# Where the second product of a SwiGLU block loads its first weights, when its operands are split, and which banks end its last token tile

## The chip, the cores and the metric

The kernel runs on one core of a Trainium2 chip. The metric is device time in microseconds of one execution, given as the median of several runs. On a core work five engines with instruction queues of their own, each in order: TensorE (PE, matmul, with PEld for the loading of its stationary operand), VectorE (DVE), ScalarE (ACT), GpSimd (POOL) and SyncE (SP, which here only issues DMA). They meet through semaphores.

## The reference, cut to what matters

One decoder block on x of 512 tokens by 1024 columns, in float32: a mixer (RWKV-7, MoBA attention and gMLP heads) and then a SwiGLU FFN with 2816 hidden columns. The change touches the end of the FFN alone:

```python
h = rmsnorm(x, pre_ffn_g[l])
gate, up = jnp.split(h @ w_ffn_in[l], 2, axis=-1)      # 512 x 2816 each
f = (jax.nn.silu(gate) * up) @ w_ffn_out[l]            # 512 x 1024: the second product
x = x + rmsnorm(f, post_ffn_g[l])
```

## The kernel before, in words

**Exactness.** Each float32 operand is split into a high part (rounded to the matmul's type, copied by ACT) and a low part (the rest, a subtraction on DVE). A product is three matmuls: high by high, high by low, low by high (`mm3`). Names that end in h and l are these parts: `wh`, `wl` of weights, `fh`, `fl` of whole blocks of f, `xh`, `xl` of quarter pieces of f.

**First product.** It makes f transposed, 22 blocks of 128 hidden columns by 512 tokens. From block 3 on, each block is computed by `seven(b, between)` with seven half-size products in place of eight, and the last part of block b (`finish`, lines 1351 to 1354: add, Silu, multiply) runs inside block b+1 as `between`. Blocks 0 to 3 are split at once into `fh` and `fl`. Blocks 4 to 21 stay whole in `bigh`, `bigl` and `fx`.

**Second product.** Its 22 rows of f blocks are in two groups. Blocks 0 to 9 are multiplied plainly, as five units of two blocks (`NU = 5`). Blocks 10 to 21 go through a scheme that replaces eight block products by seven (`product2` with the names p1 to p7, three steps u = 0, 1, 2 each). Column half 512:1024 comes first, in the order unit 0, 1, 2, 3, p1, p5, p6, unit 4, p7, p4; then half 0:512 with p2, p3 and units 0 to 4, the last three of which run token tile by token tile with `finish2` behind each tile. A unit is 24 matmuls of 128x512, a p is 36 (12 for each u).

**Weights of a step.** `w2_load` (line 1399) issues a DMA of 512 KB on SP's queue into a tile `wf`; the pools in `sp_tiles` are taken in turn, each with two buffers. `w2_parts` then copies the high part on ACT (line 1405) and subtracts the low part on DVE (line 1406). In `operands`, p5 to p3 first add or subtract two weight tiles or pieces of f on DVE (lines 1447 to 1467; `sw` is the running sum of weights, `t2` that of f) and split what they need of f into `xh` (ACT, line 1432) and `xl` (DVE, line 1433).

**Pools.** `wpool` is the old pool: the first product's weights went through it too. `fo` (the pool "out") is opened after unit 0, on memory that the first product gives back, so its first tiles wait for the last readers of that memory. Right behind `fo` the kernel appends it to `sp_tiles`, so that unit 1 loads into `wpool`, unit 2 into `fo`, unit 3 into `wpool`, p1's first step into `fo` and so on.

**Order.** PE runs in the order of the code. The other engines' instructions are placed by a list scheduler: what stands under `tc.high_priority(offset=PRI_W)` is taken as if it stood 20,000 instructions earlier. The weights' loads and splits, and those of the pieces of f, stand under it. `to_parts(b, fr[b])` for blocks 4 to 9 (lines 1277, 1278) stands in the loop over units, without precedence.

**End.** `finish2` (t is the token tile) adds the bank to what was kept in `s1` or `u2` (line 1544), squares and sums on ACT (1522), multiplies by the gain (1546), sums the squares (1549, 1551), takes the power on POOL (1554), updates x2 (1556, twice) and sends it out. The last tile, t = 3, is done in two column cuts of 256, both in the same bank `c1[1]`.

Of the kernel before, what the change touches and what calls it, by code (L numbers as in the profile page):

```python
# [12 lines left out]
OP = mybir.AluOpType  # L13
# [5 lines left out]
NB = S // 128  # L19
# [21 lines left out]
PRI_W = 20000  # L41
# [55 lines left out]
def block_kernel(ctx: ExitStack, tc: tile.TileContext, x, pre_mix_g, w_in, rwkv_mu, rwkv_w0, rwkv_w2,  # L97
# [4 lines left out]
    act, dve, pool, sp = nc.scalar, nc.vector, nc.gpsimd, nc.sync  # L102
# [22 lines left out]
    def bank(name, bufs):  # L125
        return ps.tile([128, 512], F32, name=name, bufs=bufs)

    def acc():
        return bank("acc", 2)

    def rb():
        return bank("rb", 1)

    def yb():
        return bank("yb", 1)

    def sb():
        return bank("sb", 3)
# [7 lines left out]
    def ct(shape, name, dt=F32):  # L146
        return const.tile(shape, dt, name=name)
# [244 lines left out]
    for h in range(2):  # L392
        r = slice(64 * h, 64 * h + 64)
# [74 lines left out]
    def dense_fm(free=False):  # L468

        wh, wl = feed.next()  # L470
        wh = wh.rearrange("p (k c) -> p k c", k=KB)
        wl = wl.rearrange("p (k c) -> p k c", k=KB)
        p = acc()
        for k in range(KB):
            pe.matmul(p, wh[:, k], h1[:, k], start=(k == 0), stop=False)
            pe.matmul(p, wh[:, k], l1[:, k], start=False, stop=False)
            pe.matmul(p, wl[:, k], h1[:, k], start=False, stop=(k == KB - 1))
            if free:
                od.signal("free%d" % k)
            if k < KB - 1:  # L480
                od.pump()
        return p
# [529 lines left out]
    p = dense_fm()  # L1012
# [8 lines left out]
    u2 = bkt[:, 16:24].rearrange("p u m -> p (u m)").rearrange("p (b s) -> p b s", b=2)  # L1021
# [13 lines left out]
    for b in range(2):  # L1035
        p = dense_fm(b == 1)
# [62 lines left out]
    sm = ct([128, 3 * NB], "sm")  # L1099
# [102 lines left out]
    K1, K2 = FB - 2 * NW, FB - NW  # L1202
# [9 lines left out]
    def ffn_w():  # L1212
        return tuple(w.rearrange("p (k c) -> p k c", k=KB) for w in ffeed.next())

    ws = [ffn_w() for _ in range(4)]
# [38 lines left out]
    ws = [ffn_w() for _ in range(2)]  # L1254
# [10 lines left out]
    FA = 4  # L1265
# [4 lines left out]
    fr = [h1f[:, i] for i in range(KB)] + [l1f[:, i] for i in range(KB)] + [fx[:, i] for i in range(FB - FA - 2 * KB)]  # L1270
    fr = [None] * FA + fr
# [4 lines left out]
    def to_parts(b, f):  # L1276
        act.copy(fh[b], f)
        dve.tensor_tensor(fl[b], f, fh[b].bitcast(F32), op=OP.subtract)
# [110 lines left out]
    sp_tiles, w_tiles, w2 = [wpool], [0, 0], w_ffn_out[0].rearrange("(k p) c -> p k c", p=128)  # L1389
# [19 lines left out]
    def mm3(p, ah, al, wh, wl, start, stop):  # L1409
        pe.matmul(p, ah, wh, start=start, stop=False, skip_group_check=True)  # L1410
        pe.matmul(p, ah, wl, start=False, stop=False, skip_group_check=True)
        pe.matmul(p, al, wh, start=False, stop=stop, skip_group_check=True)

    def plain_w(ui, c):
        with tc.high_priority(offset=PRI_W):
            return w2_parts(w2_load(2 * ui, c))

    def plain(ui, w, p, t, start=False, cut=slice(0, 512)):
        tk = slice(128 * t, 128 * t + 128)
        for kk in range(2):  # L1420
            b = 2 * ui + kk
            mm3(p[:, cut], fh[b][:, tk], fl[b][:, tk], w[0][:, kk, cut], w[1][:, kk, cut], start and kk == 0, kk == 1)
# [13 lines left out]
    def operands(name, u):  # L1436

        ka, kb = K1 + 2 * u, K2 + 2 * u
        b11, b12, b21, b22 = rows(ka, 0), rows(ka, 1), rows(kb, 0), rows(kb, 1)
        t2, sw = st2["t2"][u], st2["sw"][u]  # L1440
        t2v = t2.rearrange("p (k c) -> p k c", k=2)
        if name == "p1":
            a, x = w2_load(ka, 0), b11
        elif name == "p5":
            a, x = w2_load(ka, 512), b12
            other = w2_load(kb, 512)
            dve.tensor_tensor(sw, a, other, op=OP.add)  # L1447
            a = sw
        elif name == "p6":
            a = w2_load(ka, 0)  # L1450
            dve.tensor_tensor(sw, sw, a, op=OP.subtract)
            dve.tensor_tensor(t2v, b22, b12, op=OP.subtract)
            a, x = sw, t2v
        elif name == "p7":
            a, other = w2_load(ka, 0), w2_load(ka, 512)
            dve.tensor_tensor(a, a, other, op=OP.subtract)
            dve.tensor_tensor(b11, t2v, b11, op=OP.subtract)
            x = b11
        elif name == "p4":
            a = w2_load(kb, 512)  # L1460
            dve.tensor_tensor(t2v, b21, t2v, op=OP.subtract)
            x = t2v
        elif name == "p2":
            a, x = w2_load(kb, 0), b21
        else:
            a, x = w2_load(kb, 0), b22
            dve.tensor_tensor(a, a, sw, op=OP.subtract)
        return w2_parts(a), f_parts(x)

    def product2(name, ps_, start=False):  # L1470

        for u in range(NW // 2):
            with tc.high_priority(offset=PRI_W):
                w, x = operands(name, u)
            for t in range(2):
                tk = slice(128 * t, 128 * t + 128)
                for kk in range(2):
                    mm3(ps_[t], x[0][:, kk, tk], x[1][:, kk, tk], w[0][:, kk], w[1][:, kk], start and u == kk == 0,
                        u == NW // 2 - 1 and kk == 1)

    def keep_banks(name, ps_):
        with tc.high_priority(offset=2 * PRI_W):
            d = u3 if name == "u3" else st2["fo"].tile([128, 2, 512], F32, name=name)
            for t in range(2):
                act.copy(d[:, t], ps_[t])
        return d

    NU = K1 // 2
    c0, cd = (rb(), yb()), (ob(), sb())
    for ui in range(NU - 1):  # L1490
        w = plain_w(ui, 512)
        for t in range(NB):
            plain(ui, w, (c0 + cd)[t], t, ui == 0)
        if ui == 0:
            between()
            ffs.close()
            hps.close()
            fo = st2["fo"] = ph2.enter_context(tc.tile_pool(name="out", bufs=1, reuse_waits="tile"))
            sp_tiles.append(fo)
            for b in range(FA, K1):  # L1500
                fh.append(fo.tile([128, S], F32R, name="fh%d" % b))
                fl.append(fo.tile([128, S], F32R, name="fl%d" % b))
                to_parts(b, fr[b])
            st2["t2"] = [fo.tile([128, 512], F32, name="t2_%d" % u) for u in range(NW // 2)]
            st2["sw"] = [fo.tile([128, 1024], F32, name="sw%d" % u) for u in range(NW // 2)]
            raw = fo.tile([128, NB, 512], F32, name="raw")
    cb, c1 = (acc(), acc()), (sb(), sb())
    product2("p1", cb, True)
    s1 = keep_banks("s1", cb)
    product2("p5", c1, True)  # L1510
    product2("p6", cb)
    u2 = keep_banks("u2", cb)
    w = plain_w(NU - 1, 512)
# [22 lines left out]
    ca_ = (acc(), acc())  # L1536
    product2("p2", ca_, True)
    product2("p3", c1)

    def finish2(t, cut, last):  # L1540

        e = (s1, u2)[t // 2][:, t % 2]
        i = 3 * t + (1 if cut.start == 0 else 2)
        dve.tensor_tensor(e[:, cut], (ca_ + c1)[t][:, cut], e[:, cut], op=OP.add)
        square_sum(e[:, cut], i)
        dve.tensor_tensor(e[:, cut], e[:, cut], orow[:, cut], op=OP.mult)
        r = rs[:, t:t + 1]
        if cut.start == 0:
            dve.scalar_tensor_tensor(r, sm[:, i - 1:i], 1e-6, sm[:, i:i + 1], op0=OP.add, op1=OP.add)  # L1549
        else:  # L1550
            dve.tensor_tensor(r, r, sm[:, i:i + 1], op=OP.add)
        if not last:
            return
        pool.tensor_tensor(r, r, mhalf[:, 0:1], op=OP.pow)  # L1554
        for c, src in ((slice(512, D), raw[:, t]), (slice(0, 512), e)):
            dve.scalar_tensor_tensor(x2[:, t, c], src, r, x2[:, t, c], op0=OP.mult, op1=OP.add)  # L1556
            sp.dma_start(out_rows[:, t, c], x2[:, t, c])

    ws = []
    for ui in range(NU):  # L1560
        ws.append(plain_w(ui, 0))
        if ui < NU - 3:
            for t in range(NB):
                plain(ui, ws[ui], (ca_ + c1)[t], t)
    for t in range(NB):
        cuts = [slice(0, 512)] if t < NB - 1 else [slice(0, 256), slice(256, 512)]
        for cut in cuts:
            for ui in range(NU - 3, NU):
                plain(ui, ws[ui], (ca_ + c1)[t], t, False, cut)
            finish2(t, cut, cut is cuts[-1])  # L1570
    inner.close()
    ph2.close()

# [28 lines left out]
```

## Time and profile before

| what | us |
| --- | --- |
| runs | 655.35, 655.42, 657.01 |
| median | 655.42 |
| the profiled execution | 656.08 |
| its span, first to last instruction | 654.4 |
| PE busy | 631.9 (97%) |
| DVE busy | 490.0 (75%) |
| ACT busy | 326.3 (50%) |
| mean granted TensorE clock | 0.990 of full speed |

The span is the time between the first and the last instruction of the profiled execution; 1.68 us of that execution lie outside it. A busy PE means that matmuls are under way, at whichever clock; the granted clock says how fast. Of two matmuls with the same shape the difference of their starts is the time that one takes from the stream, since they overlap in the pipeline.

### The profile page before, as it was taken

The page shows a single profiled execution, that of the slowest core. Times are in us where ns is not written, and L with a number is a line of the kernel's source. Part 1 is how long each engine was busy: PE and PEld are TensorE (multiplying, and loading weights), DVE is VectorE, ACT ScalarE, POOL GpSimd, SP SyncE. Part 2 cuts the span into 40 slices and gives each one's busy share as a digit, 9 for nine tenths or more (in the row PEclk, how much of TensorE's full clock was granted, in tenths as well). Part 3 has the DMA queues.
Part 4 walks back from the last instruction along what each step waited for, and adds up shares of the span by engine and source line. Part 5 has one row for each costly group of instructions (what it writes and reads, how often), then busy time and mean ns, then how long its engine had stood idle before and what let it go on. Part 6 is the DMA issues. An engine that isn't in the chain of part 4 may idle for free.

```text
span 654.4 us, 11566 instructions
## 1 busy us (share of the span) xinstructions
PE 631.9 (97%) x4582; PEld 559.4 (85%) x4582; DVE 490.0 (75%) x834; ACT 326.3 (50%) x582; POOL 59.5 (9%) x111
## 2 busy tenths in 40 slices
PE   8998999999999999999999999999999978999995
PEld 7886879877878887789999999999999967788884
DVE  2799969886565768468988888888888565889825
ACT  6653543455554463456755455555455351646511
POOL 7021121032130100022000000000000000000001
PEclk9999999999999999999999999999999998999999
DMA  7422012321211126406333243343342144856503
GB/s 228 132 69 66 25 48 78 108 67 46 58 33 33 34 65 258 135 26 189 102 97 115 81 127 99 96 130 97 98 124 71 37 157 161 263 171 209 161 0 129
DMA packets 84981, 69.12 MB, mean 106 GB/s; under 512 B 2968, under 2 KB 70976, under 8 KB 84928
## 3 DMA queue, kind: packets, MB, share of 16 engines
q1 hardware_dynamic: 83024, 65.76, 32.4%
q10 hardware_dynamic: 1904, 2.63, 1.3%
q8 instruction: 36, 0.59, 0.4%
q14 instruction: 17, 0.14, 0.1%
HBM read 66.28 MB, written 2.10 MB: 104 GB/s over the span
## 4 chain that ended last, share of the span: by engine, by line
PE 68%; DVE 9%; DMA 4%; issue 2%; ACT 1%; POOL 0%; DVEq 0%; POOLq 0%; ACTq 0%
PE acc L112 30%; PE sb L112 27%; PE rb L112 4%; PE yb L112 3%; DMA wf<-in_w_ffn_out_dram 3%; PE ob L112 3%; PE sb L117 1%; DVE wl L185 1%; DMA wf<-in_w_out_dram 1%; DVE wl L1406 1%; ACT wh L183 1%; DVE sw L1447 1%; DVE xl L1433 1%; DVE x L1556 1%; DVE bigl L814 0%
## 5 line engine op out<-in xcount | busy, mean ns | idle before, releaser
L112 PE MATMUL sb<-h,wh 128*128 128x256 f32 x260 | 73.5, 283 | 0.0
L112 PE MATMUL sb<-h,wl 128*128 128x256 f32 x260 | 73.4, 282 | 0.0
L112 PE MATMUL sb<-l,wh 128*128 128x256 f32 x260 | 73.3, 282 | 0.0
L112 PE MATMUL acc<-bigh,wh 128*128 128x512 f32 (+1 forms) x168 | 67.0, 402 | 0.3 <-ACT bigh L281 0.3
L112 PE MATMUL acc<-bigl,wh 128*128 128x512 f32 (+1 forms) x168 | 63.6, 383 | 0.3
L183 ACT ACTIVATE wh<-wf 128x512 fp32r<-128x512 f32 (+2 forms) x60 | 40.4, 711 | 45.6 <-PE acc L112 31.6
L185 DVE TENSOR_TENSOR wl<-wf,wh 128x512 fp32r<-128x512 f32 (+2 forms) x60 | 46.6, 799 | 19.2 <-ACT wh L183 17.2
L112 PE MATMUL acc<-bigh,wl 128*128 128x512 f32 (+1 forms) x168 | 59.3, 377 | 0.0
L1313 ACT ACTIVATE wh<-wf 128x1024 fp32r<-128x1024 f32 x38 | 40.1, 1059 | 33.5 <-DVE wf L1334 16.0
L1314 DVE TENSOR_TENSOR wl<-wf,wh 128x1024 fp32r<-128x1024 f32 x38 | 46.0, 1222 | 9.6 <-ACT wh L1313 9.6
L112 PEld LDWEIGHTS sb<-l,wh 128*128 128x128 f32 x260 | 49.5, 190 | 0.0
L112 PEld LDWEIGHTS sb<-h,wh 128*128 128x128 f32 x260 | 49.5, 190 | 0.0
L112 PEld LDWEIGHTS sb<-h,wl 128*128 128x128 f32 x260 | 49.5, 190 | 0.0
L1405 ACT ACTIVATE wh<-wf 128x1024 fp32r<-128x1024 f32 x25 | 26.1, 1057 | 37.0 <-PE sb L112 29.9
L112 PEld LDWEIGHTS acc<-bigh,wh 128*128 128x128 f32 x168 | 32.0, 190 | 6.0 <-ACT bigh L281 0.6
L112 PEld LDWEIGHTS acc<-bigl,wh 128*128 128x128 f32 x168 | 31.9, 190 | 5.8 <-DVE bigl L282 0.9
L1406 DVE TENSOR_TENSOR wl<-wf,wh 128x1024 fp32r<-128x1024 f32 x25 | 30.1, 1218 | 8.2 <-ACT wh L1405 8.1
L1313 ACT ACTIVATE wh<-sums 128x1024 fp32r<-128x1024 f32 x19 | 20.1, 1060 | 31.7 <-PE acc L112 16.4
L112 PEld LDWEIGHTS acc<-bigh,wl 128*128 128x128 f32 x168 | 30.0, 189 | 6.2
L1554 POOL TENSOR_TENSOR rs<-rs,mhalf 128x1 f32<-128x1 f32 x4 | 2.2, 549 | 343.1 <-DVE rs L1549 339.3
L1314 DVE TENSOR_TENSOR wl<-sums,wh 128x1024 fp32r<-128x1024 f32 x19 | 23.2, 1223 | 13.2 <-ACT wh L1313 13.2
L112 PE MATMUL acc<-l,wh 128*128 128x256 f32 x108 | 30.5, 283 | 0.9 <-DVE l L1187 0.9
(489 smaller groups left out, 1906.8 us busy)
## 6 DMA issues: line engine op xcount, KB each, us to landing
wf<-in_w_ffn_in_dram SPq DMA_DIRECT2D x76, 256.0 KB
wf<-in_w_ffn_out_dram SPq DMA_DIRECT2D x37, 512.0 KB
wf<-in_w_in_dram SPq DMA_DIRECT2D x21, 512.0 KB
wf<-in_w_out_dram SPq DMA_DIRECT2D x8, 512.0 KB
wf<-in_w_ffn_in_dram SPq DMA_DIRECT2D x6, 512.0 KB
xt<-in_x_dram SPq DMA_DIRECT2D x4, 512.0 KB
x<-in_x_dram SPq DMA_DIRECT2D x4, 512.0 KB
out_dram<-x SPq DMA_DIRECT2D x8, 256.0 KB
```

The lines of the kernel that those rows point to most:

```text
L112: return nc.tensor.matmul(out_, lhsT, rhs, **kw)
L117: return nc.tensor.transpose(out_, in_, idn)
L183: act.activation(h[:, c], t[:, c], AF.Copy)
L185: eng.tensor_tensor(l[:, c], t[:, c], h[:, c].bitcast(F32), op=OP.subtract)
L1313: act.activation(h, src, AF.Copy)
L1314: dve.tensor_tensor(l, src, h.bitcast(F32), op=OP.subtract)
L1405: act.activation(h, src, AF.Copy)
L1406: dve.tensor_tensor(l, src, h.bitcast(F32), op=OP.subtract)
L1433: dve.tensor_tensor(l, src, h.bitcast(F32), op=OP.subtract)
L1447: dve.tensor_tensor(sw, a, other, op=OP.add)
L1554: pool.tensor_tensor(r, r, mhalf[:, 0:1], op=OP.pow)
L1556: dve.scalar_tensor_tensor(x2[:, t, c], src, r, x2[:, t, c], op0=OP.mult, op1=OP.add)
```

## The change

Three edits, all in the second product.

1. `sp_tiles.append(fo)` moves out of the loop over units, behind it. Units 0 to 3 thus all load into `wpool`; `fo` takes part from p1 on.
2. `to_parts` of blocks 4 to 7 (the f blocks of units 2 and 3) gets the precedence PRI_W, ahead of the splits of p1's pieces in the code. Blocks 8 and 9 (unit 4) are split behind `product2("p5")` in the code, with the same precedence.
3. The last three units of token tile 3 no longer add to bank `c1[1]`: the first column cut starts a sum of its own in a bank from `rb()`, the second in one from `yb()`. What the earlier work left in `c1[1]` is added to `u2[:, 1]` by one new DVE instruction (line 1571 after the change) ahead of the loop over tiles. The line that adds the second cut's square sum moves within `finish2`.

```diff
-            sp_tiles.append(fo)
             for b in range(FA, K1):
                 fh.append(fo.tile([128, S], F32R, name="fh%d" % b))
                 fl.append(fo.tile([128, S], F32R, name="fl%d" % b))
-                to_parts(b, fr[b])
+            with tc.high_priority(offset=PRI_W):
+                for b in range(FA, 2 * NU - 2):
+                    to_parts(b, fr[b])
...
+    sp_tiles.append(fo)
     cb, c1 = (acc(), acc()), (sb(), sb())
     product2("p1", cb, True)
     s1 = keep_banks("s1", cb)
     product2("p5", c1, True)
+    with tc.high_priority(offset=PRI_W):
+        for b in range(2 * NU - 2, K1):
+            to_parts(b, fr[b])
     product2("p6", cb)
...
-    def finish2(t, cut, last):
+    def finish2(t, p, cut, last):
...
-        dve.tensor_tensor(e[:, cut], (ca_ + c1)[t][:, cut], e[:, cut], op=OP.add)
+        dve.tensor_tensor(e[:, cut], p[:, cut], e[:, cut], op=OP.add)
...
+    with tc.high_priority(offset=PRI_W):
+        dve.tensor_tensor(u2[:, 1], c1[1], u2[:, 1], op=OP.add)
     for t in range(NB):
-        cuts = [slice(0, 512)] if t < NB - 1 else [slice(0, 256), slice(256, 512)]
-        for cut in cuts:
+        end = t == NB - 1
+        cuts = [slice(0, 256), slice(256, 512)] if end else [slice(0, 512)]
+        for cut, p in zip(cuts, (rb(), yb()) if end else (ca_ + c1)[t:t + 1]):
             for ui in range(NU - 3, NU):
-                plain(ui, ws[ui], (ca_ + c1)[t], t, False, cut)
-            finish2(t, cut, cut is cuts[-1])
+                plain(ui, ws[ui], p, t, end and ui == NU - 3, cut)
+            finish2(t, p, cut, cut is cuts[-1])
```

Lines behind the first edit have other numbers after the change: `finish2`'s 1544, 1546, 1549, 1551, 1556 become 1549, 1551, 1554, 1558, 1561.

**SP's queue, the loads of units 1 to 3 and of p1 and p5.** Before (wf_5993 is unit 1, wf_6053 unit 3, wf_6023 unit 2, wf_6087, wf_6109 and wf_6131 are p1's three steps, wf_6156 and wf_6158 the pair of p5's first step, wf_6181 and wf_6183 that of its second):

```order
L1399 DMA wf_5993<-in_w_ffn_out_dram 128x2x512
L1399 DMA wf_6053<-in_w_ffn_out_dram 128x2x512
L1399 DMA wf_6109<-in_w_ffn_out_dram 128x2x512
L1399 DMA wf_6023<-in_w_ffn_out_dram 128x2x512
L1399 DMA wf_6087<-in_w_ffn_out_dram 128x2x512
L1399 DMA wf_6156<-in_w_ffn_out_dram 128x2x512
L1399 DMA wf_6131<-in_w_ffn_out_dram 128x2x512
L1399 DMA wf_6158<-in_w_ffn_out_dram 128x2x512
L1399 DMA wf_6181<-in_w_ffn_out_dram 128x2x512
```

After (wf_5989 is unit 1, wf_6019 unit 2, wf_6049 unit 3, wf_6083, wf_6105 and wf_6127 are p1's steps, wf_6152 and wf_6154 the pair of p5's first step, wf_6177 the first of its second):

```order
L1399 DMA wf_5989<-in_w_ffn_out_dram 128x2x512
L1399 DMA wf_6019<-in_w_ffn_out_dram 128x2x512
L1399 DMA wf_6049<-in_w_ffn_out_dram 128x2x512
L1399 DMA wf_6105<-in_w_ffn_out_dram 128x2x512
L1399 DMA wf_6083<-in_w_ffn_out_dram 128x2x512
L1399 DMA wf_6127<-in_w_ffn_out_dram 128x2x512
L1399 DMA wf_6152<-in_w_ffn_out_dram 128x2x512
L1399 DMA wf_6154<-in_w_ffn_out_dram 128x2x512
L1399 DMA wf_6177<-in_w_ffn_out_dram 128x2x512
```

Unit 2's load moved from the fourth place to the second, into the buffer of unit 0; unit 3's from the second to the third.

**ACT, the high parts of the weights of units 1 to 3 and what follows.** Before (wh_5995 is unit 1, wh_6055 unit 3, wh_6025 unit 2, wh_6089 p1's first step):

```order
L1374 COPY grow_3596<-acc_5800 128x256
L1405 ACTIVATE wh_5995<-wf_5993 128x1024
L1352 ACTIVATE frow_2920<-frow_2920 128x512
L1379 COPY u3_5802<-acc_5800 128x256
L1405 ACTIVATE wh_6055<-wf_6053 128x1024
...
L1277 CAST fh9_5982<-bigh_3594 128x512
L1352 ACTIVATE frow_2920<-frow_2920 128x512
L1391 DMA grow_5894<-in_post_ffn_g_dram 128x1024
L1405 ACTIVATE wh_6025<-wf_6023 128x1024
L1405 ACTIVATE wh_6089<-wf_6087 128x1024
```

After (wh_6021 is unit 2, wh_5991 unit 1, wh_6051 unit 3, wh_6085 p1's first step):

```order
L1405 ACTIVATE wh_6021<-wf_6019 128x1024
L1374 COPY grow_3596<-acc_5800 128x256
L1405 ACTIVATE wh_5991<-wf_5989 128x1024
L1352 ACTIVATE frow_2920<-frow_2920 128x512
L1379 COPY u3_5802<-acc_5800 128x256
L1405 ACTIVATE wh_6051<-wf_6049 128x1024
...
L1277 CAST fh9_5972<-bigh_3594 128x512
L1352 ACTIVATE frow_2920<-frow_2920 128x512
L1391 DMA grow_5894<-in_post_ffn_g_dram 128x1024
L1405 ACTIVATE wh_6085<-wf_6083 128x1024
```

Unit 2's copy moved from behind the splits of f (the last of them fh9) to a place ahead of unit 1's, before a copy of the first product's last block (1374).

**DVE, the low parts behind unit 3's weights.** Before:

```order
L1406 TENSOR_TENSOR wl_6056<-wf_6053,wh_6055 128x1024
L1433 TENSOR_TENSOR xl_6094<-bigh_3594,xh_6093 128x512
L1433 TENSOR_TENSOR xl_6116<-bigl_3595,xh_6115 128x512
L1433 TENSOR_TENSOR xl_6138<-bigl_3595,xh_6137 128x512
L1433 TENSOR_TENSOR xl_6166<-bigh_3594,xh_6165 128x512
L1278 TENSOR_TENSOR fl4_5963<-bigh_3594,fh4_5962 128x512
L1457 TENSOR_TENSOR bigh_3594<-t2_0_5986,bigh_3594 128x2x256
L1278 TENSOR_TENSOR fl5_5967<-bigh_3594,fh5_5966 128x512
```

After:

```order
L1406 TENSOR_TENSOR wl_6052<-wf_6049,wh_6051 128x1024
L1278 TENSOR_TENSOR fl4_5963<-bigh_3594,fh4_5962 128x512
L1278 TENSOR_TENSOR fl5_5965<-bigh_3594,fh5_5964 128x512
L1278 TENSOR_TENSOR fl6_5967<-bigh_3594,fh6_5966 128x512
L1278 TENSOR_TENSOR fl7_5969<-bigh_3594,fh7_5968 128x512
L1433 TENSOR_TENSOR xl_6090<-bigh_3594,xh_6089 128x512
L1433 TENSOR_TENSOR xl_6112<-bigl_3595,xh_6111 128x512
```

The low parts of f for units 2 and 3 moved ahead of the four pieces of p1 and p5.

## Rows read from the trace of the kernel before

**Rows 1.** Busy time by stretch: PE, PEld, DVE, ACT, POOL, clock, DMA share, GB/s.

```profile
535.00:541.70 6.70, 0.71 (x2) 0.19 (x1) 6.70 (x12) 4.18 (x6) 0.00 (x0) 0.84 0.23 84
541.70:546.20 4.50, 4.48 (x11) 3.52 (x12) 3.53 (x4) 0.00 (x0) 0.00 (x0) 0.50 0.65 204
546.20:640.00 93.80, 93.55 (x406) 76.00 (x405) 64.71 (x74) 42.36 (x60) 0.55 (x1) 1.00 0.50 163
```

**Rows 2.** Timeline of PE: start, us, instruction, idle time before it and releaser.

```profile
534.82 0.40 PE L112 MATMUL sb<-wh,fl 128*128 128x512 f32 x1
537.34 0.49 PE L112 MATMUL rb<-wh,fh 128*128 128x512 f32 x1 [2.13 <-ACT wh L1405]
541.72 0.79 PE L112 MATMUL rb<-wl,fh 128*128 128x512 f32 x1 [3.88 <-DVE wl L1406]
...
546.47 0.40 PE L112 MATMUL ob<-wh,fh 128*128 128x512 f32 x1
...
571.32 0.40 PE L112 MATMUL acc<-wh,xh 128*128 128x512 f32 x1
571.97 0.50 PE L112 MATMUL acc<-wl,xh 128*128 128x512 f32 x1 [0.25 <-DVE wl L1406]
...
580.18 0.39 PE L112 MATMUL rb<-wh,fh 128*128 128x512 f32 x1
```

**Rows 3.** Waits of SP's queue, 494 to 530: total, times, longest.

```profile
SPq L1399 <- PE sb L112: 7.1, 1, 7.1
```

**Rows 4.** Timeline of SP's queue: when loads were issued.

```profile
509.25 0.37 SPq L1399 DMA_DIRECT2D wf<-in_w_ffn_out_dram  x1
...
529.55 0.37 SPq L1399 DMA_DIRECT2D wf<-in_w_ffn_out_dram  x1
```

**Rows 5.** Timeline of ACT around the first units.

```profile
517.01 0.37 ACT L1374 COPY grow<-acc 128x256 f32<-128x256 f32 x1 [3.93 <-PE acc L112]
...
529.56 1.06 ACT L1405 ACTIVATE wh<-wf 128x1024 fp32r<-128x1024 f32 x1 [7.80 <-PE sb L112]
...
532.59 3.22 ACT L1277 CAST fh<-bigh 128x512 fp32r<-128x512 f32 x6
...
536.25 2.94 ACT L1405 ACTIVATE wh<-wf 128x1024 fp32r<-128x1024 f32 x3
```

**Rows 6.** Timeline of DVE from unit 2 to p6.

```profile
537.44 2.49 DVE L1278 TENSOR_TENSOR fl<-bigh,fh 128x512 fp32r<-128x512 f32 x4
...
540.45 3.49 DVE L1406 TENSOR_TENSOR wl<-wf,wh 128x1024 fp32r<-128x1024 f32 x3
...
547.58 1.23 DVE L1447 TENSOR_TENSOR sw<-wf 128x1024 f32<-128x1024 f32 x1 [2.31 <-DMA wf<-in_w_ffn_out_dram]
553.93 1.23 DVE L1447 TENSOR_TENSOR sw<-wf 128x1024 f32<-128x1024 f32 x1 [5.13 <-DMA wf<-in_w_ffn_out_dram]
...
558.82 1.23 DVE L1447 TENSOR_TENSOR sw<-wf 128x1024 f32<-128x1024 f32 x1 [2.53 <-DMA wf<-in_w_ffn_out_dram]
...
574.78 1.22 DVE L1406 TENSOR_TENSOR wl<-sw,wh 128x1024 fp32r<-128x1024 f32 x1
```

**Rows 7.** Chain that ended last, 534 to 582: start, us, what.

```profile
548.83 5.01 DMA wf<-in_w_ffn_out_dram
...
560.08 5.14 DMA wf<-in_w_ffn_out_dram
```

**Rows 8.** Timeline of PE in the last token tile.

```profile
644.35 0.28 PE L112 MATMUL sb<-wh,fl 128*128 128x256 f32 x1
645.41 0.39 PE L112 MATMUL sb<-wh,fh 128*128 128x256 f32 x1 [0.78 <-DVE u L1544]
```

**Rows 9.** Timeline of DVE from the first to the last token tile.

```profile
634.20 0.69 DVE L1544 TENSOR_TENSOR s<-acc,s 128x512 f32<-128x512 f32 x1 [7.44 <-PE acc L112]
...
647.35 0.15 DVE L1549 SCALAR_TENSOR_TENSOR rs<-sm 128x1 f32<-128x1 f32 x1
647.84 0.42 DVE L1544 TENSOR_TENSOR u<-sb,u 128x256 f32<-128x256 f32 x1 [0.33 <-PE sb L112]
```

More of the change, by code (lines that the diff above doesn't have):

```diff
@@ L1549, in finish2 @@
             dve.scalar_tensor_tensor(r, sm[:, i - 1:i], 1e-6, sm[:, i:i + 1], op0=OP.add, op1=OP.add)
-        else:
-            dve.tensor_tensor(r, r, sm[:, i:i + 1], op=OP.add)
         if not last:
             return
+        if cut.start:
+            dve.tensor_tensor(r, r, sm[:, i:i + 1], op=OP.add)
         pool.tensor_tensor(r, r, mhalf[:, 0:1], op=OP.pow)
```

## The prediction, made before the changed kernel ran

> **What bounds the kernel now.** I read the busy shares by stretch first, then PE's timeline, then the queues that PE waits for. PE is 97% busy, so what counts is where it is idle or slow. In the second product the stretches show three pieces [rows 1]: from 535.0 to 541.7 PE has two matmuls, from 541.7 to 546.2 it runs at a granted clock of 0.50 (1.2 of 2.4 GHz), and from there to 640 it is busy at 1.00 (2.4 GHz), with 93.80 us for 406 matmuls, 0.231 us each. PE's timeline names the causes [rows 2]. Unit 1's last matmul starts at 534.82 and its successor could start at 535.05. Unit 2 starts at 537.34, waiting for ACT's high part of its weights; its second matmul waits for DVE's low part until 541.72; the next eleven steps take 546.47 - 541.72 = 4.75 us where 11 x 0.231 = 2.54 would do. Later p6's second matmul waits, 571.97 - 571.32 - 0.23 = 0.42. The pieces: 2.29 + (541.72 - 537.34 - 0.23 = 4.15) + 2.21 + 0.42 = 9.07. The whole stretch says the same: from 535.05 to unit 4's start at 580.18 are 45.13 us for 156 matmuls (units 2 and 3, p1, p5, p6), worth 36.04; the loss is 9.1.
>
> Why unit 2's weights are late: SP waits 7.1 us for PE before it may use `fo`'s memory [rows 3], so the load is issued at 529.55, while unit 3's went out at 509.25 into `wpool` [rows 4]. Unit 3 was split first, at 529.56 [rows 5]. Behind it ACT's queue holds all splits of f, then three weight copies in a row from 536.25 (unit 2's first) [rows 5]; DVE's queue the same, with three low parts from 540.45, unit 2's first [rows 6]. So it was not the transfer's length: unit 2's load went out 7 us before ACT took it up, and unit 2 stood last in two queues.
>
> **The change, part by part.**
>
> *Loads.* Unit 2 takes the slot of 509.25. Two loads in the chain of waits took 5.01 and 5.14 us [rows 7], so it lands near 514.5. Its copy stands in ACT's queue ahead of the copy of line 1374, which ran at 517.01 after 3.93 us of idle time, waiting for PE [rows 5]. The copy is one third of 2.94, 1.0 us: 514.5 to 515.5, inside that idle time. DVE subtracts for 1.16 us (3.49 / 3) to about 516.7. PE needs it at 535.05. This costs nothing while ACT is idle there; if the load landed after 516, line 1374's copy, the bank that it frees and PE behind it would be late by as much. Unit 3's load goes into unit 2's buffer when that low part is done, near 516.7, and lands near 522, ahead of its split, which stays at 529.56 for the same event of PE [rows 5]. `fo`'s first two buffers go to p1's first and third step, at 529.55 and behind it.
>
> *Precedence.* The high parts of four f blocks (3.22 / 6 = 0.54 us each) now start at about 530.5 on ACT, behind unit 3's copy, and the low parts (2.49 / 4 = 0.62 each) follow unit 3's low part on DVE. That ends near 532.5: before, eight instructions of this size (four of line 1433, two of 1278, two of 1457) lay between it and the row of 537.44 [rows 6], and 537.44 - 8 x 0.62 = 532.5. Blocks 4 and 5 are then ready at 533.1 and 533.7, 6 and 7 by 535.0; PE needs the low parts of 4 and 5 at 535.5 and 536.2 (third and sixth matmul of unit 2) and the others with unit 3 at 540.6. The pieces of p1 come behind them, from 537.5, and are needed at 546. So unit 2's wait goes to about zero, at most 0.3 us.
>
> *What is late next: DVE.* It must have p6's last low part ready before PE gets there. Before, from 540.45 to 576.00 (574.78 + 1.22) are 35.55 us, of which 2.31 + 5.13 + 2.53 = 9.97 are waits for weights at the three sums of p5 [rows 6]; the work is 25.6. After the change one low part of 1.16 is done long before, so that piece is ready at 540.45 + 25.6 - 1.16 = 564.9 plus the new waits W. PE, without stall, reaches it 24 + 120 matmuls after 535.05, at 568.3. W up to 3.4 therefore costs nothing. My W: the pair for p5's second step is the last to be late. Its second load was issued only after the first sum (547.58 to 548.81), at 548.83, since it shared that buffer [rows 6, 7]. Now its buffer is that of p1's third step, free with that low part at 540.45 + 3 x 1.16 + 0.6 for a t2 = 544.5; with 4.9 us, a little under the two loads of rows 7, it lands at 549.4. DVE would reach it at 546.3 (544.5, 0.6 for line 1457, 1.2 for the first sum). W is 3.1, the piece is ready at 568.0, 0.3 ahead of PE. Third pair: issued before 547, landed by 552, reached by DVE at 553.5: no wait. With 5.5 us for that load PE would wait 0.4. I take a slip of 0.3, between 0 and 0.5, for this and unit 2's first matmul.
>
> *Last tile.* PE's second cut waits for DVE to read the shared bank: it starts 645.41 - 644.35 = 1.06 behind its predecessor instead of 0.12 (half of 0.231, for half the width), so 0.94 is lost [rows 8]. With two banks PE ends 0.94 earlier. DVE, which waits for that with 0.33 idle, is busy until 647.35 + 0.15 = 647.50 and starts the last addition at 647.84 [rows 9]. So the end moves by 0.34 to 0.42, not by 0.94; I take 0.4. The new addition of 128x512 costs 0.69, the row of the same shape at 634.20, and lies in the 7.44 us of idle time ahead of that row [rows 9]; without that cover it would cost 0.69. Moving the second square sum changes no instruction.
>
> The rows thus show a DVE that is the next limit in the last tile. The Trainium skill, "Perfetto Trace Analysis", section "Optimizing Tensor Performance / Matmuls", says that independent matmul groups should rotate through PSUM banks so that one group's evacuation overlaps the next one's matmuls. By that alone the tail would gain the whole wait of PE, 0.94; by rows 9 it gains 0.4.
>
> *Sum.* 9.1 - 0.3 + 0.4 = 9.2. The profiled execution of 656.08 becomes 646.9; it stands 0.66 above the median of 655.42, which becomes 646.2.
>
> **The rivals.**
>
> *B: the weight chain binds in p5 and p6.* The waits at the second and third sum stay as long as they were, 5.13 + 2.53 = 7.7, because p5's six loads, now up to 9 us closer to PE's need, come at the same rate. Then p6's last low part is ready at 564.9 + 7.7 = 572.6, PE waits 4.3, and the gain is 9.1 - 4.3 + 0.4 = 5.2: 650.2; with W in between, 646.2 to 650.2. If the clock fell again over that pause, 2.2 more. For it: a slack of 0.3 us is small, and before the change DVE waited here three times. Against it: the load behind the longest of these waits, 5.13, no longer stands behind the first sum.
>
> *C: it doesn't do what it says.* Unit 2 still waits as before, because its early copy or the splits of f come as late as they did. Only the tail is left: 655.42 - 0.4 = 655.0. For it: the splits of f still stand behind unit 3's copy, which waits for PE until 529.56, so block 4 is ready only 2.4 us before PE needs it. Against it: unit 2's weights are out of this queue altogether, and they were what PE waited for in both rows of the stall.
>
> *D: slower, through buffers.* DVE's waits stay at all three sums, W = 10. The piece is ready at 574.9, PE waits 6.6 in three pauses (p5's first, its last, p6's last step), and each pause lets the clock fall to half for another 2.2, as the one at 541.7 did [rows 1]: 6.6 + 6.6 = 13.2 against 9.5 gained, +3.7: 659.1. With all three falls it decides from W = 3.4 + (9.5 - 6.6) = 6.3 on. Against it: the short pause of 0.42 at 571.97 let no clock fall [rows 1, 2], and no load of p5 is issued later than before.
>
> The Trainium skill, "Perfetto Trace Analysis", section "Optimization Strategy" under "Identifying Performance Opportunities", reads gaps that repeat along a stretch as a possible lack of buffers. That speaks against a change that gives four units two buffers instead of up to four, and by it D is what would be seen; of the traces only the three repeated waits of DVE in rows 6 bear it out, and those loads keep their buffers.
>
> **How the numbers follow.** Forecast (stall gone, DVE just ahead): 0.72. B: 0.18. C: 0.06. D: 0.04. The low end is the forecast without slip and with the whole 0.94 of the tail: 655.42 - 9.1 - 0.94 = 645.4, less 0.2 for the sum's own rounding: 645.2. The high end is B's bound, 650.2; outside stay C, D and B with a clock fall. A measurement of this kernel can tell about 0.3% from no change, 2.0 us. Faster by more: the forecast and B, 0.90. Within: C, 0.06. Slower: D, 0.04.
>
> **What would show it.** In the changed kernel's trace: unit 2's high part on ACT near 514.5 and before line 1374's copy; no PE gap between 534.8 and 546 over 0.3 us and a clock of 1.00 there; p1 starting near 546.1, p6 near 562.8, unit 4 near 571.1 to 571.6; DVE's waits for weights together about 3 and p6's last low part at about 568; the last cut's first matmul 0.12 behind its predecessor, and DVE's last addition with no wait for PE ahead of it. Wrong it would be if PE waits for DVE in p5 or p6 by more than 0.5 (B), if PE still waits at unit 2 (C), if the clock row shows 0.50 after 541 (D), or if line 1374's copy comes later than 517.3.

## The result, and the profile after

The changed kernel takes 648.0 us (median of 4 runs, 647.45 to 648.14) against 655.5 (4 runs) of the kernel before; the ratio is 0.9875 (95% interval 0.9859 to 0.9891). Five later runs of it have a median of 647.75 against 655.99, ratio 0.9866 (0.9847 to 0.9885). The forecast was 646.2, in a range of 645.2 to 650.2. The profiled execution took 647.45, its span is 645.4 where 654.4 stood. The span is thus 9.0 shorter and the execution 8.6, since 2.05 us of it lie outside the span where 1.68 did. That difference is there in every run: 1.67 to 1.80 of the kernel before, 2.03 to 2.10 of the changed one. The edits alone do not make it, since a kernel with all three of them and 3.6 us more work (below) has 1.69 to 1.77; its cause is open.

The stretches that answer to [rows 1], with the columns of that group, and one more:

```profile
535.00:541.70 6.70, 6.70 (x30) 5.42 (x29) 6.70 (x12) 4.12 (x6) 0.00 (x0) 1.00 0.24 90
541.70:546.20 4.50, 4.50 (x22) 3.70 (x21) 4.50 (x5) 0.17 (x1) 0.00 (x0) 1.00 0.67 206
546.20:575.00 28.80, 28.80 (x127) 23.51 (x126) 24.46 (x28) 16.55 (x22) 0.00 (x0) 1.00 0.71 242
575.00:632.00 57.00, 56.66 (x247) 45.84 (x246) 38.88 (x46) 25.06 (x37) 0.55 (x1) 1.00 0.43 138
```

Where PE had two matmuls in 6.7 us and then a clock of 0.50, it now runs without a gap at 1.00, with 30 and 22 matmuls. DVE is busy for all 6.70 us from 535.0 to 541.7, before and after: what changed there is the order of its work. One gap is new, the 0.34 us that are missing between 575 and 632.

PE's timeline (start, us, instruction, idle time before it and releaser), answering to [rows 2]:

```profile
534.81 0.40 PE L112 MATMUL sb<-wh,fl 128*128 128x512 f32 x1
535.04 0.39 PE L112 MATMUL rb<-wh,fh 128*128 128x512 f32 x1
...
571.00 0.39 PE L112 MATMUL rb<-wh,fh 128*128 128x512 f32 x1
...
584.77 0.40 PE L112 MATMUL rb<-wh,xh 128*128 128x512 f32 x1
585.50 0.50 PE L112 MATMUL rb<-wl,xh 128*128 128x512 f32 x1 [0.34 <-DVE wl L1406]
```

Unit 2 follows unit 1 by 0.23 us, unit 4 starts at 571.00 instead of 580.18. The new gap stands at p4's first step: its second matmul comes 0.73 behind its first, 0.50 more than the 0.23 of a matmul, and waits for DVE's low part.

Unit 2's weights on SP's queue, ACT and DVE, answering to [rows 4] and [rows 5]:

```profile
509.24 0.37 SPq L1399 DMA_DIRECT2D wf<-in_w_ffn_out_dram  x1
516.35 0.37 SPq L1399 DMA_DIRECT2D wf<-in_w_ffn_out_dram  x1
```

```profile
514.00 1.06 ACT L1405 ACTIVATE wh<-wf 128x1024 fp32r<-128x1024 f32 x1 [0.93 <-PE sb L112]
517.00 0.37 ACT L1374 COPY grow<-acc 128x256 f32<-128x256 f32 x1 [1.94 <-PE acc L112]
```

```profile
515.09 1.22 DVE L1406 TENSOR_TENSOR wl<-wf,wh 128x1024 fp32r<-128x1024 f32 x1 [1.66 <-ACT wh L1405]
...
532.61 2.49 DVE L1278 TENSOR_TENSOR fl<-bigh,fh 128x512 fp32r<-128x512 f32 x4
...
549.57 1.23 DVE L1447 TENSOR_TENSOR sw<-wf 128x1024 f32<-128x1024 f32 x1 [3.26 <-DMA wf<-in_w_ffn_out_dram]
...
566.28 1.22 DVE L1406 TENSOR_TENSOR wl<-sw,wh 128x1024 fp32r<-128x1024 f32 x1
```

The split of unit 2 lies in idle time of both engines, 20 us ahead of its use; the copy of line 1374 stays at 517.00. SP still waits 7.1 us for `fo`'s memory, but the load behind that wait, at 529.54, is now one of p1, which has time. Of DVE's three waits for the sums of p5 [rows 6] one is left, 3.26 us. The last low part of p6 is ready at 567.5.

The last tile, PE and DVE, answering to [rows 8] and [rows 9]:

```profile
635.79 0.28 PE L112 MATMUL rb<-wh,fl 128*128 128x256 f32 x1
635.91 0.28 PE L112 MATMUL yb<-wh,fh 128*128 128x256 f32 x1
```

```profile
621.48 0.69 DVE L1571 TENSOR_TENSOR u<-sb,u 128x512 f32<-128x512 f32 x1 [3.27 <-PE sb L112]
...
638.79 0.15 DVE L1554 SCALAR_TENSOR_TENSOR rs<-sm 128x1 f32<-128x1 f32 x1
638.87 0.41 DVE L1549 TENSOR_TENSOR u<-yb,u 128x256 f32<-128x256 f32 x1
```

The second cut follows at 0.12 us, and DVE's last addition stands directly behind its own earlier work, with no wait for PE.

**Where the time went, by kernel.** Executions differ by up to 1.2 us before 90 us of the trace, long before the change (on this the last section). So kernels are compared from a mark behind that: the start of the first product's last 24 matmuls, behind unit 0 (526.60 before, 526.59 after). The table gives the starts' distances in us, as the traces have them: from the mark to unit 4 (units 1 to 3, p1, p5, p6), from there to p4 (unit 4, p7), p4, from p2 to PE's last matmul, and from that to the end of the span. The span is given to a tenth, so a difference between two rows of the last column, or of the sum, can be off by 0.1.

| kernel | to unit 4 | to p4 | p4 | p2 to last matmul | to the end | sum |
| --- | --- | --- | --- | --- | --- | --- |
| before | 53.58 | 13.78 | 8.26 | 45.30 | 6.88 | 127.80 |
| after | 44.41 | 13.77 | 8.89 | 44.27 | 7.47 | 118.81 |
| after, again | 44.41 | 13.78 | 9.26 | 44.27 | 7.50 | 119.22 |
| first edit alone | 46.52 | 13.78 | 8.26 | 45.75 | 6.86 | 121.17 |
| second edit alone | 54.43 | 13.78 | 8.26 | 45.34 | 6.85 | 128.66 |
| third edit alone | 53.62 | 13.77 | 8.27 | 44.27 | 7.41 | 127.34 |
| without the second edit | 45.76 | 13.78 | 8.26 | 44.76 | 7.50 | 120.06 |
| after, p4's load first | 44.41 | 13.77 | 8.26 | 44.27 | 7.48 | 118.19 |
| after, multiplication apart | 44.41 | 13.77 | 9.07 | 44.28 | 6.79 | 118.32 |
| after, both | 44.41 | 13.77 | 8.26 | 44.40 | 6.85 | 117.69 |
| after, 3.6 us more on DVE | 48.48 | 13.81 | 8.26 | 44.27 | 7.43 | 122.25 |

From before to after: -9.17 up to unit 4, +0.63 in p4 (+1.00 in the second profile), -1.03 for PE's last stretch, +0.59 behind it (the rounding of the span allows 0.1). The end follows DVE: from p2's start to DVE's last addition are 45.62 before (602.22 to 647.84) and 45.21 after (593.66 to 638.87), 0.41 less.

### The profile page after: what moved, and what is told of

It reads as the page before. It is cut to its first block, busy times and chain, and to the rows that moved or that the text cites. A ratio compares the mean times of both kernels' runs of the same rounds, so it can differ in the third digit from the quotient of the medians.

```text
span 645.4 us, 11568 instructions
## 1 busy us (share of the span) xinstructions
PE 627.0 (97%) x4582; PEld 555.7 (86%) x4582; DVE 490.1 (76%) x835; ACT 326.5 (51%) x582; POOL 59.5 (9%) x111
## 4 chain that ended last, share of the span: by engine, by line
PE 66%; DVE 11%; DMA 3%; issue 3%; ACT 2%; POOL 0%; DVEq 0%; POOLq 0%; ACTq 0%
PE acc L112 28%; PE sb L112 27%; PE rb L112 4%; PE yb L112 3%; PE ob L112 2%; DMA wf<-in_w_ffn_out_dram 2%; DVE wl L1406 2%; PE sb L117 1%; DVE wl L185 1%; DMA wf<-in_w_out_dram 1%; DVE xl L1433 1%; ACT wh L183 1%; DVE fl L1278 1%; DVE x L1561 1%; DVE bigl L814 0%
```

## The experiments

**The changed kernel once more.** No edit.

> The changed kernel once more, unaltered. Its first profiled execution took 647.45 us at a mean granted clock of 0.999; three other executions took 647.98 to 648.14 at 0.994. Theory: the 0.6 us between them lie at p4's first step, where PE waited 0.5 us for DVE in the profiled one; there a slower load (4.13 us there) makes the wait longer and the clock falls behind it. Expected of a profile with 0.994: a PE gap over 1 us at p4 and a stretch below 1.00 behind it. Rival: the difference lies elsewhere (the first product, or after PE's end), and p4's gap is again 0.5.

647.75 us (646.89 to 648.93). PE's wait at p4 was longer, and its chain reads, in order of time (start, us, what):

```profile
579.98 4.60 DMA wf<-in_w_ffn_out_dram
...
584.60 1.07 ACT wh L1405
...
585.70 1.24 DVE wl L1406
```

```profile
586.98 0.50 PE L112 MATMUL rb<-wl,xh 128*128 128x512 f32 x1 [0.71 <-DVE wl L1406]
```

In the first profile the transfer took 4.13 us, here 4.60. The gap is over 1 us (585.87 to 586.98) as the theory had it, but the clock was 1.00 behind it. The lower mean clock comes from the stretch of 60 to 70 us (last section), and the mark of the table is 1.1 us late already (527.68 against 526.59), far ahead of the change. The rival is right in that.

**One edit at a time.** The first edit alone:

```diff
-            sp_tiles.append(fo)
...
+    sp_tiles.append(fo)
     cb, c1 = (acc(), acc()), (sb(), sb())
```

> The first edit alone: units 0 to 3 load into the old pool, no precedence for blocks 4 to 9, last tile as before. Theory (unit 2's weights were the stall, the splits of f only follow): units 2 and 3 run but for 0.7 us, since the low part of block 5 now ends near 536.9 where PE needs it at 536.2; span about 646.4 and time about 647.2 to 648.5. Rival (the order of the splits of f carries half of the gain): time about 651, PE waiting for DVE's low parts of f at unit 2 for 4 us.

649.32 us (648.09 to 650.72), ratio 0.9894 (0.9875 to 0.9914). The stall at unit 2 is gone with this edit alone: 46.52 to unit 4 instead of 53.58. What remains against the whole change are 2.1 us. From unit 2's start to unit 3's 6.43 instead of 5.57, since the low parts of blocks 4 and 5 come late, and 1.29 in p6:

```profile
537.90 0.50 PE L112 MATMUL rb<-wh,fl 128*128 128x512 f32 x1 [0.24 <-DVE fl L1278]
565.56 0.50 PE L112 MATMUL acc<-wl,xh 128*128 128x512 f32 x1 [0.73 <-DVE wl L1406]
```

The second is rival B of the prediction, in a place and with a size of its own: DVE waits 0.86, 2.27 and 2.89 for the three sums' weights, 6.0 together, where 3.4 had been worked out as what costs nothing.

```profile
556.27 1.23 DVE L1447 TENSOR_TENSOR sw<-wf 128x1024 f32<-128x1024 f32 x1 [2.89 <-DMA wf<-in_w_ffn_out_dram]
```

The second edit alone:

```diff
-                to_parts(b, fr[b])
+            with tc.high_priority(offset=PRI_W):
+                for b in range(FA, 2 * NU - 2):
+                    to_parts(b, fr[b])
...
+    with tc.high_priority(offset=PRI_W):
+        for b in range(2 * NU - 2, K1):
+            to_parts(b, fr[b])
```

> The second edit alone: blocks 4 to 7 split ahead of p1's pieces, loads as before. Theory: unit 2's weights are still loaded from 529.55 and split behind all of f, so PE waits at unit 2 as before (2.1 and 3.9 us, clock 0.50 behind it): 655.0 to 655.7, ratio 1.000. Rival: 651.

656.23 us, ratio 1.0002 (0.999 to 1.0013): nothing. Its one trace is 0.85 longer up to unit 4, which the runs don't bear out as a loss: 0.51 of it lie between unit 2's start and unit 3's, where the clock fell earlier (the first matmul of unit 2 lasts 0.80, not 0.49), and 0.37 in p6, where PE's wait for the low part was longer. The two waits at unit 2 are those of [rows 2]:

```profile
538.48 0.80 PE L112 MATMUL rb<-wh,fh 128*128 128x512 f32 x1 [2.12 <-ACT wh L1405]
542.86 0.79 PE L112 MATMUL rb<-wl,fh 128*128 128x512 f32 x1 [3.59 <-DVE wl L1406]
```

The third edit alone (the last part of the diff of the change, nothing else):

> The third edit alone: the last tile in two banks of its own. Theory: 0.4 us, since DVE is busy until 647.5 of the trace before; last addition with no wait for PE ahead of it; span 654.0. Rival: PE's whole wait of 0.94 comes back: span 653.4.

655.71 us, ratio 0.9993 (0.9982 to 1.0005). PE's last stretch is shorter by 1.03, what follows it longer by 0.53; the sum is 0.46 less than before. From p2's start (602.32) to DVE's last addition are 45.21, the same 0.41 less as in the whole change. DVE's rows show why it is not 0.94: the last addition is behind DVE's own work, as in the prediction.

```profile
647.46 0.15 DVE L1549 SCALAR_TENSOR_TENSOR rs<-sm 128x1 f32<-128x1 f32 x1
647.53 0.41 DVE L1544 TENSOR_TENSOR u<-yb,u 128x256 f32<-128x256 f32 x1
```

**What the precedence is worth beside the first edit.** The changed kernel with the second edit undone:

> The changed kernel without the second edit (blocks 4 to 9 split without precedence), so that the difference to the changed kernel is the precedence alone. In the run with the first edit alone PE lost 2.1 us more up to unit 4 than with the whole change: 0.9 at unit 2, where the low parts of blocks 4 and 5 came late, and 1.3 at p6, behind a wait of DVE of 2.9 for the weights of the third sum. Theory (only the 0.9 belongs to the missing precedence; the wait at the third sum came from one late transfer): from unit 0 to unit 4 45.3 us against 44.4, time about 648.6. Rival (the other order of the splits also puts p5's second low part behind the third sum and makes p6 late each time): 46.5 us, time 649.5 to 650.

649.34 us (648.61 to 650.12) against 647.75: 1.6 us in the medians. To unit 4 45.76, so 1.35 more than with it: the same 0.86 at unit 2, and 0.53 in p6. The theory was wrong to call p6's part one late transfer; it came again, smaller. DVE waited 0.89, 2.08 and 2.27 for the sums:

```profile
554.51 1.23 DVE L1447 TENSOR_TENSOR sw<-wf 128x1024 f32<-128x1024 f32 x1 [2.27 <-DMA wf<-in_w_ffn_out_dram]
```

Without the precedence the low part of p5's second step stands behind the third sum in DVE's row, and with it all of p6 behind that sum's wait. Its size differs between the two profiles (1.29, 0.53) with that wait. Behind p2 the kernel without the precedence is 0.49 longer too (44.76 against 44.27), and the one with the first edit alone 0.45 (45.75 against 45.30 before): PE waits in p3's third step, here the row without the precedence.

```profile
608.78 0.50 PE L112 MATMUL sb<-wl,xh 128*128 128x512 f32 x1 [0.19 <-DVE wl L1406]
```

But p4 takes 8.26 in both, as before the change. PE's new wait at p4 is thus the second edit's, made beside the first, and takes back 0.63 to 1.00 of what that edit brings; by the table's sums 0.8 to 1.25 are left. That two edits which are worth 6.6 and nothing alone bring 8.2 to 8.6 together (the table's sums, without the tail) is thus shown; that the order of DVE's row alone makes the 0.53 was not tried apart.

**The new wait at p4.** One line ahead of p4 moves the turn of the two pools by one, so that p4's first step takes the buffer that p4's second step took:

```diff
+    w_tiles[0] += 1
     product2("p4", c0)
```

> The changed kernel, with the turn of the two pools moved by one ahead of p4, so that p4's first step takes the buffer that comes free first and its load is issued ahead of those of p4's second step and p2. Theory (PE's new wait at p4, 0.5 us in one profile and 0.9 in the other, is only the place of that load in SP's queue): the wait is gone, from unit 0 to p4's end 0.5 to 0.9 us less, time 647.0 against 647.75. Rival (DVE as a whole is behind there): the wait moves to p4's second step or to p2, time as with the change, 647.7.

647.32 us (4 runs, 646.59 to 648.43), ratio 0.9864 (0.9846 to 0.9882), which the runs can't tell from the change. The trace can: p4 takes 8.26 us as before the change, and nothing behind it is longer.

```profile
585.89 0.39 PE L112 MATMUL rb<-wh,xh 128*128 128x512 f32 x1
586.12 0.40 PE L112 MATMUL rb<-wl,xh 128*128 128x512 f32 x1
```

So the 0.5 to 0.9 us were the place of one load. In the changed kernel DVE's row has the subtraction for p7's third step ahead of the low part of its second; that subtraction waited 2.67 us for its weights, and the low part behind it, done at 578.97, frees the buffer for p4's first load:

```profile
576.59 1.23 DVE wf L1456
577.82 1.15 DVE wl L1406
...
578.98 4.13 DMA wf<-in_w_ffn_out_dram
...
583.13 1.07 ACT wh L1405
...
584.23 1.24 DVE wl L1406
...
585.50 1.42 PE rb L112 x5
```

Before the change, the low part stood ahead of that subtraction, which waited too (DVE):

```profile
581.73 1.21 DVE L1406 TENSOR_TENSOR wl<-wf,wh 128x1024 fp32r<-128x1024 f32 x1
...
585.63 1.23 DVE L1456 TENSOR_TENSOR wf<-wf 128x1024 f32<-128x1024 f32 x1 [2.09 <-DMA wf<-in_w_ffn_out_dram]
```

So it does without the second edit (575.29 and 579.17 there), where p4 has no wait either.

**What ends the last tile.** The last tile's multiplication by the gain writes to a buffer that is free by then, so that it need not wait for ACT's square of the same data:

```diff
-        dve.tensor_tensor(e[:, cut], e[:, cut], orow[:, cut], op=OP.mult)
+        o = s1[:, 0] if t == NB - 1 else e
+        dve.tensor_tensor(o[:, cut], e[:, cut], orow[:, cut], op=OP.mult)
...
-        for c, src in ((slice(512, D), raw[:, t]), (slice(0, 512), e)):
+        for c, src in ((slice(512, D), raw[:, t]), (slice(0, 512), o)):
```

> The changed kernel, with the multiplication by the gain in the last token tile writing to a buffer of its own, so that it need not wait until ACT has squared its input. Theory (behind PE's end only DVE's row of work and its waits for ACT count): the last addition starts 0.3 earlier, since the first cut's multiplication fills DVE's wait for POOL, and the chain behind it is 0.3 shorter; from PE's last matmul to the end of the span 0.6 less, 647.1. Rival (the chain is ACT's and POOL's, not DVE's): 0 to 0.2.

647.44 us (4 runs), ratio 0.9861 (0.9843 to 0.9879). The last instruction of DVE, in the changed kernel and here:

```profile
641.74 0.74 DVE L1561 SCALAR_TENSOR_TENSOR x<-u,rs,x 128x512 f32<-128x512 f32 x1
...
642.29 0.75 DVE L1562 SCALAR_TENSOR_TENSOR x<-s,rs,x 128x512 f32<-128x512 f32 x1
```

It starts 3.81 behind PE's last matmul in the changed kernel (637.93) and 3.18 here (639.11): 0.6 gained, half of it ahead of the last addition and half behind it, as the theory says. (The table's 7.47 and 6.79 differ by 0.68, with the span's rounding in it.) The times of the runs do not tell the two kernels apart.

**Both together.**

> Both of these in one kernel. Theory: the two lie one behind the other on the path, 0.5 to 0.9 and 0.6 add up: 646.3 to 646.6. Rival: one of them is swallowed: 647.1.

647.16 us (5 runs, 646.08 to 649.47), ratio 0.9863 (0.9842 to 0.9885). By the table 117.69, so 1.1 to 1.5 less than the two profiles of the change, and both parts are there (8.26 and 6.85). By the runs' medians the gain is 0.6, within their spread. It is the shortest of all by the trace; that it is faster than the change is not shown by the times.

**How near DVE is.** Six repetitions of one subtraction of 0.6 us, spread from p1's weights to the third sum:

```diff
+    with tc.high_priority(offset=2 * PRI_W):
+        for _ in range(6):
+            dve.tensor_tensor(fl[9], fr[9], fh[9].bitcast(F32), op=OP.subtract)
```

> The changed kernel with six repetitions of one subtraction on DVE (block 9's low part, 0.6 us each, 3.6 in all) spread from p1's weights to the third sum of p5. Theory (DVE is the next limit, with 0.7 us to spare at p6's last low part and up to one repetition hidden in its wait for the second sum's weights): PE waits 1.6 to 2.5 us in p5 and p6, and if the clock falls behind those waits as it did at unit 2, up to 2.2 more: 649.5 to 652. Rival (DVE waits for loads anyway and has room): 0 to 0.5 us, 647.7 to 648.2.

652.35 us (651.35 to 652.57), ratio 0.9935 (0.9921 to 0.9949). 4.07 more to unit 4 for 3.6 us of work, in two waits of PE; the clock stays at 1.00 in both stretches (columns as in [rows 1]):

```profile
562.35 0.50 PE L112 MATMUL sb<-wl,xh 128*128 128x512 f32 x1 [1.04 <-DVE wl L1406]
573.38 0.50 PE L112 MATMUL acc<-wl,xh 128*128 128x512 f32 x1 [2.48 <-DVE wl L1406]
```

```profile
560.00:565.00 5.00, 3.96 (x18) 2.93 (x17) 5.00 (x7) 2.15 (x3) 0.00 (x0) 1.00 0.93 340
570.00:575.00 5.00, 2.52 (x11) 1.75 (x11) 5.00 (x7) 1.26 (x3) 0.00 (x0) 1.00 0.76 230
```

DVE is the next limit, more sharply than expected (1.6 to 2.5 without a fall of the clock). The room of 0.7 us (p6's last low part is ready at 567.5 in the changed kernel, PE there at 568.2) was used up by another change of the order as well: p6's last low part now stands behind a low part of later weights, of 1.13. With it 3.6 + 1.13 - 0.7 = 4.0, near the 4.07.

```profile
570.37 1.22 DVE L1406 TENSOR_TENSOR wl<-wf,wh 128x1024 fp32r<-128x1024 f32 x1
...
572.10 1.22 DVE L1406 TENSOR_TENSOR wl<-sw,wh 128x1024 fp32r<-128x1024 f32 x1
```

## Why the prediction was right, point by point

- *The stall and its cause.* Right. 9.1 us were put at units 2 to p6, 9.17 came back. That unit 2's place in the queues was the cause, and not the splits of f, is shown by the edits alone: the loads' pool brings 7.06 up to unit 4, the precedence alone nothing. One detail was off: unit 2's copy started at 514.00 behind a wait for PE. Its load had landed by 512.3, 3.1 us after its issue, where the prediction had counted 5 and 514.5.
- *Precedence.* Right in the sum, but it was not priced by itself. Behind the first edit it is worth 1.35 to 2.1 us up to unit 4, 0.86 of it at unit 2, and 0.5 in p3; at p4 it costs 0.6 to 1.0.
- *DVE next.* Right: W was put at 3.1 and is 3.26; p6's last low part, put at 568.0, is ready at 567.5, with PE there at 568.2. The slip of 0.3 did not come.
- *The last tile.* Right: 0.4 forecast, 0.41 at DVE's last addition, with the whole change and with the third edit alone. PE's own gain is 1.03, and 0.6 of it is lost behind PE. The Trainium skill ("Perfetto Trace Analysis", "Optimizing Tensor Performance / Matmuls") has independent matmul groups rotate through PSUM banks so that evacuation overlaps matmuls; PE's rows agree, its second cut no longer waits (0.12 behind its predecessor), but the time follows DVE.
- *The step that was missing.* The walk of DVE's queue ended at unit 4. Ahead of p4 the second edit had changed its order too, and the wait of rival B's kind came there, 0.5 us in one profile and 0.9 in the other (p4's own time is 0.63 and 1.00 longer). With it the sum would have been 9.1 + 0.4 - 0.6 to 1.0 = 8.5 to 8.9; the table has 8.99 and 8.58.
- *From the profile to the median.* The prediction took the 0.66 between the profiled execution and the median of before as the same for both kernels. For the changed one the profiled execution was 0.55 below its median. These 1.2 are the larger part of the 1.8 us between 646.2 and 648.0; 0.4 more lie outside the span, which the prediction took as unchanged, and 0.2 in the span (p4's 0.6, less the slip of 0.3 that did not come and 0.1 elsewhere). That 648.0 lies in the range owes something to the width that rival B gave it; what bears the mechanism out are the rows of the traces.
- *Rivals.* B's mechanism exists (first edit alone, 1.29 at p6), but not in the whole change. C fell. D's price fell with the last experiment, the one with 3.6 us more on DVE: PE paused 1.04 and 2.48 us there and the clock did not fall. The Trainium skill ("Perfetto Trace Analysis", "Optimization Strategy") reads gaps that repeat on the engine that should be saturated as a possible lack of buffers. That did not come either: with two buffers for four units PE shows no such gaps, and DVE's three waits for the sums' weights became one, of 3.26.

## What to carry to other kernels

When an operand is late, look at its place in each queue that it passes, not only at its transfer: here a load left 20 us earlier by borrowing a buffer that was free, and its split fell into idle time of two engines. After such a move follow the next engine's queue to the end of the kernel, not to the end of the repaired stretch, since a list scheduler rearranges what comes behind. An edit that is worth nothing alone can gain beside another, and cost elsewhere, so test edits both ways.

## What the runs showed of the hardware

The granted clock did not follow the length of one pause. With 3.6 us more on DVE, PE paused 2.48 us at 573.38 and ran on at 1.00; before the change the waits of 2.13 and 3.88, one matmul between them, were followed by 0.50 [rows 1, 2]. And the same pause of the same kernel can go either way. In the mixer, at the start of the kernel, PE waits for DVE near 63 us, and the stretch around it (columns as in [rows 1]) is at 1.00 in the first profile of the changed kernel and at 0.83 in the second:

```profile
63.04 0.46 PE L112 MATMUL rb<-ar,bk 64*128 64x128 f32 x2 [1.75 <-DVE bk L577]
```

```profile
60.00:70.00 10.00, 8.07 (x59) 6.29 (x58) 8.44 (x14) 3.66 (x6) 0.41 (x1) 1.00 0.19 54
```

```profile
63.16 0.46 PE L112 MATMUL rb<-ar,bk 64*128 64x128 f32 x2 [1.77 <-DVE bk L577]
```

```profile
60.00:70.00 10.00, 8.06 (x51) 6.13 (x50) 7.44 (x12) 3.49 (x6) 0.00 (x1) 0.83 0.18 54
```

What decides it stays open. Nor does it explain alone the 1.2 us by which executions differ at the mark: the profile of before has 0.83 there too, and its mark at 526.60, and the one with both additions has 1.00 and its mark at 527.71.
